# Split-weight rings of four tiles and a second raw ring in the up projections

## The chip, the cores and the metric

The kernel runs on one core of a Trainium2 chip. The metric is the time of one execution on the device in microseconds (us), the median of several runs; smaller is better. The core has a matrix engine (TensorE, PE in the profile), a vector engine (VectorE, DVE), a scalar engine (ScalarE, ACT), GpSimd (POOL, hardly used here) and SyncE (SP), which here issues DMA loads. Each engine works off its own instructions in order; semaphores hold an instruction until what it needs is there.

## The reference

Two layers of a transformer-like trunk on a sequence of 1024 tokens, width 1024, in float32. Layer 0 mixes tokens with a gated short convolution, layer 1 with latent attention; both have the same kind of MLP, and the change lies in its first half:

```python
def squared_relu_mlp(h, w_up, w_down):      # w_up 1024 x 4096, w_down 4096 x 1024
    return jnp.square(jax.nn.relu(h @ w_up)) @ w_down

for l in range(DEPTH):                      # DEPTH = 2
    ...
    h = modulate(rmsnorm(x, norm_g[l, 2]), sh_f, sc_f)
    y = squared_relu_mlp(h, mlp_up_w[l], mlp_down_w[l])
    x = x + g_f[:, None, :] * rmsnorm(y, norm_g[l, 3])
```

## The kernel before

All large products run on TensorE in a reduced float format, and each float32 operand is split in two halves: `hi` is the rounded copy (ScalarE, `split_w`, L176) and `lo` the rest (VectorE, L177). A product takes three matmuls per 128 x 512 tile (`mm`, L173): lo by hi, hi by lo, hi by hi.

The up projection `h @ w_up` is worked off in 16 pairs of 128-column blocks of `w_up`. A pair is a 2 x 2 block product by Winograd's form of Strassen's scheme: seven block products in place of eight. Each block product is four tiles deep, so it is 12 matmuls. In the code the products have numbers. A later pair (`begun is None`) runs first the blocks "11" and "21", then P6, P7, P5, P3 and P4; that makes 84 matmuls. For the pairs 0 to 4 (`AHEAD = 5`), the products "11" and "21" have been done ahead, in `first_pairs`, while the residual of the previous stage was still being finished, and five products, 60 matmuls, are left. Pair 0 is worked off wholly in `first_pairs`, under an order written out by hand (`ORDER`, inside `pinned()`, which fixes the order on all engines but SP); the pairs 1 to 15 run in `all_pairs`.

What a pair needs in tiles:

- Two raw weight tiles a and b (128 x 1024 float32, 4 KB a partition), loaded by `load_pair` through SP. They come from `raw_tile()`, a ring of four that is shared with everything else that is loaded: the residual's tiles in the stage before, the modulation weights `ada_w` (`ada_acc`, L198, run in the background by `run_bg`), the activations of the next stage.
- Split tiles `uphi` and `uplo` from `up_split`, rings of three each in the pool `up`. `pair_sums` makes in this order: two differences and sums on VectorE in the raw tiles (L526, L527), the split t2 of raw tile b, the difference L531, the split s2 (its own pair of half-size tiles, one buffer), the difference L534, and the split t3 of raw tile a. A later pair makes one more split, of the unmodified a. P6 uses s2, P5 and P4 use t2, P7 and P3 use t3. A raw tile is free when its last split has been made, a split tile when its last product has run.
- PSUM banks: `x_` collects P6, P5 and P3 in this order, `v` P7 and P4. Between two of these, what is in `x_` must be taken out (`take`): on VectorE in L580 for the pairs 1 to 4, on ScalarE in L578 for the later ones. P3 and P4 of a pair are kept back in the list `end` and run within the next pair (`second`, `fourth`); a later pair runs them after its products "11" and "21", whereas the pairs 2 to 4 run them after their own P6.

Outside of `pinned()` blocks a planner of the framework puts the instructions of each engine in order before the program runs: by the order of the program, and by when it reckons that operands, tiles and buffers will be ready. A ring's size therefore decides both how long an instruction waits on the chip and where the planner puts it. The results of a pair are squared and combined (`store`, `sums`, L1189 to L1207) and stored to the DRAM tiles `ha` or `hd` for the down projection.

The pool `up` is opened in `down_phase` (used with `pairs=True` in front of both up projections, and with `pairs=False` in front of the attention, where `up` carries the weights of the query and key projections) and released at the end of `mlp_up`; the down projection (`down_pairs`) then lays its weight tiles over that place.

Of the kernel before, what the change touches and what calls it, by code (L numbers as in the profile page):

```python
# [8 lines left out]
F32 = mybir.dt.float32  # L9
F32R = mybir.dt.float32r  # L10
# [7 lines left out]
P = 128  # L18
D = 1024
S = 1024  # L20
KD = D // P
# [14 lines left out]
AHEAD = 5  # L36
# [25 lines left out]
def trunk_kernel(ctx: ExitStack, tc: tile.TileContext, x, c, ada_w, ada_b, norm_g, conv_in_w, conv_w,  # L62
# [5 lines left out]
    def nm(s):  # L68
        uid[0] += 1
        return f"{s}_{uid[0]}"  # L70
# [32 lines left out]
    def raw_tile():  # L103
        return rawp.tile([P, D], F32, tag="raw", name=nm("raw"), bufs=4)
# [4 lines left out]
    def row_tile():  # L109
        return yp.tile([P, D], F32, tag="y", name=nm("y"), bufs=NT)  # L110
# [15 lines left out]
    def ld(out_, in_):  # L126
        nc.sync.dma_start(out_, in_)
# [47 lines left out]
    def split_w(hi, lo, src):  # L175
        nc.scalar.activation(hi, src, AF.Copy)  # L176
        nc.vector.tensor_tensor(lo, src, hi.bitcast(F32), op=ALU.subtract)  # L177
# [328 lines left out]
        return up_split(up, r3, kk)  # L506

    def up_split(up, r3, kk=KD):
        hi = up.tile([P, KD, P], F32R, tag="uphi", name=nm("uphi"), bufs=3)
        lo = up.tile([P, KD, P], F32R, tag="uplo", name=nm("uplo"), bufs=3)  # L510
        split_w(hi[:, :kk, :], lo[:, :kk, :], r3[:, :kk, :])
        return hi, lo


    def load_pair(w, i):
        raws = []
        for f in (2 * i, 2 * i + 1):
            raw = raw_tile().rearrange("p (k m) -> p k m", k=KD)
            ld(raw, w[:, f * P:(f + 1) * P].rearrange("(k p) m -> p k m", p=P))
            raws.append(raw)  # L520
        return raws
# [22 lines left out]
    def halves(t):  # L544
        return t[:, :HALF], t[:, HALF:]
# [97 lines left out]
    def first_pairs(seam, acts, up, wmat, ws, ops):  # L643

        acts = {**acts, **seam.acts(PLAIN)}
        tiles, ca, wl, rest, out_, seen = {}, {}, {}, {}, {}, {}

        def late(i):
            wl[i] = ad.tile([P, D], F32, tag="acc", name=nm("w"), bufs=1).rearrange("p (k m) -> p k m", k=KD)
            ld(wl[i], wmat[:, 2 * i * P:(2 * i + 1) * P].rearrange("(k p) m -> p k m", p=P))  # L650

        def narrow():
            if not tiles:
                banks(True)
                tiles.update({i: bank_ps() if i > 1 else mm_ps() for i in range(AHEAD)})

        def first(i):
            narrow()
            prod(tiles[i], (ws[i], 0, "11"), ops)

        def first_out(i):
            ca[i] = row_tile()
            nc.scalar.activation(ca[i][:, HALF:], tiles[i], AF.Copy)

        def second(i):
            prod(tiles[i], (ws[i], 4, "21"), ops, False)

        def second_out(i):
            nc.scalar.activation(ca[i][:, :HALF], tiles[i], AF.Relu)

        def high(r3, part_=None):
            hi, lo = part_ or (up.tile([P, KD, P], F32R, tag="uphi", name=nm("uphi"), bufs=3),
                               up.tile([P, KD, P], F32R, tag="uplo", name=nm("uplo"), bufs=3))
            nc.scalar.activation(hi, r3, AF.Copy)
            return hi, lo

        def low(w, r3):
            nc.vector.tensor_tensor(w[1], r3, w[0].bitcast(F32), op=ALU.subtract)

        def split_late(i):  # L680
            low(ws[i], wl[i])
            if i + 1 < AHEAD:
                late(i + 1)

        for i in range(AHEAD):
            acts[f"fi{i}"] = lambda i=i: first(i)
            acts[f"ev1_{i}"] = lambda i=i: first_out(i)
            acts[f"se{i}"] = lambda i=i: second(i)
            acts[f"ev2_{i}"] = lambda i=i: second_out(i)
            acts[f"spa{i}"] = lambda i=i: ws.append(high(wl[i]))  # L690
            acts[f"spd{i}"] = lambda i=i: split_late(i)
        late(3)
        a, b = load_pair(wmat, 0)
        a11, a12, a21, a22 = a[:, 0:4, :], a[:, 4:8, :], b[:, 0:4, :], b[:, 4:8, :]
        sums = {}

        def diff(dst, x_, y_, op=ALU.subtract):
            nc.vector.tensor_tensor(dst, x_, y_, op=op)

        def begin():  # L700
            diff(a11, a11, a21)
            diff(a21, a21, a22, ALU.add)

        def s2():
            sums["s2"] = high(a21, tuple(up.tile([P, 4, P], F32R, tag="s2" + "hl"[i], name=nm("s2"), bufs=1) for i in range(2)))

        acts["S1"] = begin
        acts["t2a"] = lambda: sums.update(t2=high(b))
        acts["t2d"] = lambda: low(sums["t2"], b)
        acts["S2"] = lambda: diff(a21, a22, a11)  # L710
        acts["s2a"] = s2
        acts["S3"] = lambda: diff(a12, a12, a21)
        acts["s2d"] = lambda: low(sums["s2"], a21)
        acts["t3a"] = lambda: sums.update(t3=high(a))
        acts["t3d"] = lambda: low(sums["t3"], a)

        def piece(j, kk):
            w, k0, name = {5: ("t2", 0, "t1"), 4: ("t2", 4, "t4"), 6: ("s2", 0, "t2"), 7: ("t3", 0, "t3"), 3: ("t3", 4, "22")}[j]
            if j not in out_:
                out_[j] = mm_ps() if j in (5, 6) else bank_ps()  # L720
            seen[j] = seen.get(j, 0) + 1
            w = sums[w]
            mm(out_[j], (w[0][:, k0 + kk, :], w[1][:, k0 + kk, :]), ops[name][kk], seen[j] == 1, seen[j] == 4)

        for j in (3, 4, 5, 6, 7):
            for kk in range(4):
                acts[f"p{j}_{kk}"] = lambda j=j, kk=kk: piece(j, kk)

        with pinned():
            for name in ORDER:  # L730
                acts[name]()
            p1, cb = ca[0][:, HALF:], row_tile()
            c21, c22 = halves(cb)
            nc.vector.tensor_tensor(c21, p1, out_[6], op=ALU.add)
            nc.vector.tensor_tensor(c22, c21, out_[5], op=ALU.add)
            nc.vector.tensor_tensor(c21, c21, out_[4], op=ALU.add)
            nc.vector.tensor_tensor(p1, c22, out_[3], op=ALU.add)
            nc.vector.tensor_tensor(c22, c22, out_[7], op=ALU.add)
            nc.vector.tensor_tensor(c21, c21, out_[7], op=ALU.add)
        return [ca[i] for i in range(AHEAD)], cb  # L740
# [415 lines left out]
    def down_phase(slots, sizes, wd, src_fn, g, xsrc, xdst, next_w, key, ys=None, pairs=True):  # L1156

        begun = ys is not None
        ys = ys or [row_tile() for _ in range(NT)]
        up = pool("up", "right")  # L1160
        ws = []
        seam = Seam(nx, ys, vtile[g], xsrc, xdst)
        if pairs:
            names = ("11", "21", "22", "t1", "t2", "t3")
            hs = {n: as_quarter(slots[i]) for n, i in zip(names, (2, 3, 0, 1, 4, 5))}
            hs["t4"] = {}
            acts, steps0 = quarter_steps(ys, key, hs), None
            wcols = [next_w[:, 2 * i * P:(2 * i + 1) * P] for i in range(3)]
        else:
            hs = [as_h(slots, H0), as_h(slots, H1)]  # L1170
            steps0, steps1 = h_steps(tp, ys, 0, key, hs[0]), h_steps(tp, ys, 1, key, hs[1])
            wcols = [next_w[:, i * P:(i + 1) * P] for i in range(3)]
        down(slots, sizes, wd, src_fn, ys, seam, steps0, 0, lambda: ws.extend(up_weights(up, [w]) for w in wcols), begun)
        if pairs:
            return up, ws, hs, first_pairs(seam, acts, up, next_w, ws, hs), ys
        return up, ws, hs, first_block(seam, steps0, steps1, ws, hs[0]), ys

    def mlp_up(l, up, ops, firsts, per_pair_bg):

        ca, cb = firsts  # L1180
# [34 lines left out]
        def between(i):  # L1215
            flush()
            if i >= AHEAD:
                run_bg(per_pair_bg)

        store(0, ca[0], cb)  # L1220
        end = all_pairs(up, ops, [(lambda i=i: load_pair(mlp_up_w[l], i), ca[i] if i < AHEAD else None, quarter,
                                   lambda a, b, i=i: store(i, a, b), lambda i=i: between(i)) for i in range(1, n)])
        second, fourth = end.pop(), end.pop()
        second()
# [6 lines left out]
    def cols_of(w, n):  # L1231
# [5 lines left out]
    up, ws, hs, firsts, _ = down_phase(slots, (2, 2, 4), conv_out_w[0], from_dram(hd), "g0m", x0, xs[0],  # L1237
                                      mlp_up_w[0], "0f")
# [9 lines left out]
    up, ws, hs, firsts, ys = down_phase(slots, (ROWS,), mlp_down_w[0], from_dram(hd), "g0f", xs[0], xs[1], q_a_w[0], "1m", ys=ys,  # L1248
                                       pairs=False)
# [253 lines left out]
    for h in range(H):  # L1503
# [58 lines left out]
        if more:  # L1562
            keys(K2, kw, h + 1, 0)
            queries(Q2, qw_, 0)
            if h % 2:
                rotary(R2, qw_, 0)
                V2 = {}
                for b in range(4):
# [17 lines left out]
    up, ws, hs, firsts, _ = down_phase(slots, (2, 2, 4), attn_o_w[0], from_dram(hd), "g1m", xs[1], xs[2],  # L1586
                                      mlp_up_w[1], "1f")
# [52 lines left out]
```

## Time and profile before

| | us |
|---|---|
| median of 3 runs | 2179.61 (2178.7 to 2180.36) |
| the profiled execution | 2180.9 |
| its span, first to last instruction | 2179.1 |
| TensorE busy | 2098.4 (96%) |
| VectorE busy | 1512.0 (69%) |
| ScalarE busy | 1062.7 (49%) |

The mean granted clock of TensorE is 0.993 of full speed. The DMA queue of loads moved 248.57 MB. In the rows of the profile a name like `uplo<-raw,uphi` gives what an instruction writes and reads, by the names of the program's tiles; x121 is a count; "idle before" is the time in which the engine stood still just before such instructions, and what ended it. `raw` is a raw weight tile, `uphi` and `uplo` the split tiles, `s` the split s2, `y` a row tile with results, `one`, `mm` and `tp` PSUM banks, `slot` and `q` the split activations.

### The profile page before, as it was taken

The numbers are of one execution on the slowest core, as the hardware profiler recorded it, in microseconds if no ns is written. First come the engines' busy times: TensorE is split into PE (matmuls) and PEld (weight loads), VectorE is DVE, ScalarE is ACT, GpSimd is POOL, SyncE is SP. The second block draws the span as 40 slices with busy tenths as digits, with TensorE's granted clock in tenths as the row PEclk, the third lists the DMA queues.
The fourth block names the chain that finished last, engine by engine and source line by source line (L and its number), as shares of the span: only waits on it lengthen the run. The fifth ranks groups of instructions, "written<-read, shape, count | busy, mean of one in ns | idle before, by whom it ended". The sixth has DMA issues, their size and how long they took to land.

```text
span 2179.1 us, 25354 instructions
## 1 busy us (share of the span) xinstructions
PE 2098.4 (96%) x9702; PEld 1726.9 (79%) x9702; DVE 1512.0 (69%) x2001; ACT 1062.7 (49%) x1512; POOL 4.0 (0%) x8
## 2 busy tenths in 40 slices
PE   6999999989999999999899999999989999999998
PEld 5888878768888778888777888877768887788887
DVE  5877776967665578956788776665966665458556
ACT  4533354735454434344665555564735444444342
POOL 0000000000000000000000000000000000000000
PEclk9999999999999999999999999999999999999999
DMA  8344463346543977444224131053345553853243
GB/s 243 101 147 134 145 212 127 101 146 203 184 160 120 330 262 254 167 147 170 78 69 122 66 113 44 25 164 122 98 149 174 183 188 119 312 196 126 97 145 135
DMA packets 242335, 330.95 MB, mean 152 GB/s; under 512 B 18629, under 2 KB 143906, under 8 KB 242214
## 3 DMA queue, kind: packets, MB, share of 16 engines
q1 hardware_dynamic: 204328, 248.57, 35.8%
q10 hardware_dynamic: 37886, 80.77, 9.8%
q8 instruction: 76, 1.25, 0.2%
q14 instruction: 45, 0.37, 0.1%
HBM read 248.55 MB, written 80.74 MB: 151 GB/s over the span
## 4 chain that ended last, share of the span: by engine, by line
PE 69%; DVE 14%; ACT 8%; DMA 6%; issue 2%; SPq 0%; ACTq 0%; DVEq 0%
PE one L173 34%; PE mm L173 18%; PE tp L173 7%; PE big L173 4%; DMA raw<-in_ada_w_dram 3%; ACT junk L258 2%; PE big L1433 2%; DVE y L318 1%; DVE raw L319 1%; DVE acc L198 1%; PE tp L1459 1%; DVE uplo L177 1%; DMA raw<-ha 1%; DVE y L312 1%; ACT small L260 1%
## 5 line engine op out<-in xcount | busy, mean ns | idle before, releaser
L173 PE MATMUL one<-slot,uphi 128*128 128x512 f32 x1240 | 383.9, 391 | 0.0
L173 PEld LDWEIGHTS one<-slot,uphi 128*128 128x128 f32 x1240 | 233.8, 189 | 48.6 <-issue 0.5
L173 PE MATMUL big<-slot 128*128 128x512 f32 x1152 | 266.5, 391 | 1.0 <-ACT y L884 0.6
L173 PE MATMUL one<-slot,uplo 128*128 128x512 f32 x620 | 244.1, 394 | 14.6 <-DVE y L580 12.6
L173 PEld LDWEIGHTS big<-slot 128*128 128x128 f32 x1152 | 215.9, 188 | 46.7 <-ACT y L884 1.4
L173 PE MATMUL one<-ring,ring 128*128 128x512 f32 x1008 | 232.3, 391 | 6.5 <-DVE ring L177 6.5
L177 DVE TENSOR_TENSOR uplo<-raw,uphi 128x1024 fp32r<-128x1024 f32 x121 | 145.8, 1221 | 130.5 <-ACT uphi L176 130.5
L176 ACT ACTIVATE ring<-w 128x1024 fp32r<-128x1024 f32 x98 | 103.7, 1058 | 261.7 <-PE tp L173 132.1
L173 PEld LDWEIGHTS one<-ring,ring 128*128 128x128 f32 x1008 | 188.2, 188 | 49.5 <-ACT ring L176 5.8
L176 ACT ACTIVATE uphi<-raw 128x1024 fp32r<-128x1024 f32 x121 | 128.2, 1060 | 143.8 <-PE one L173 91.6
L177 DVE TENSOR_TENSOR ring<-w,ring 128x1024 fp32r<-128x1024 f32 x98 | 119.8, 1222 | 109.7 <-ACT ring L176 109.6
L173 PE MATMUL mm<-ring,ring 128*128 128x512 f32 x672 | 162.4, 390 | 0.0
L173 PE MATMUL tp<-ring,ring 128*128 128x512 f32 x672 | 161.7, 389 | 0.0
L173 PE MATMUL mm<-slot,uphi 128*128 128x512 f32 x504 | 158.5, 395 | 0.0
L173 PEld LDWEIGHTS one<-slot,uplo 128*128 128x128 f32 x620 | 116.8, 188 | 43.6 <-DVE y L580 15.1
L173 PEld LDWEIGHTS mm<-ring,ring 128*128 128x128 f32 x672 | 125.7, 188 | 27.1 <-DVE ring L177 0.6
L173 PEld LDWEIGHTS tp<-ring,ring 128*128 128x128 f32 x672 | 126.2, 188 | 26.2
L198 DVE SCALAR_TENSOR_TENSOR acc<-raw,csil,acc 128x1024 f32<-128x1024 f32 x88 | 112.8, 1282 | 45.7 <-DMA raw<-in_ada_w_dram 42.2
L177 DVE TENSOR_TENSOR ring<-raw,ring 128x1024 fp32r<-128x1024 f32 x98 | 119.4, 1219 | 18.3 <-ACT ring L176 18.3
L173 PE MATMUL one<-slot,s 128*128 128x512 f32 x468 | 115.1, 395 | 3.7 <-DVE s L177 3.7
L578 ACT ACTIVATE y<-one 128x512 f32<-128x512 f32 x62 | 36.7, 592 | 159.3 <-PE one L173 104.7
L173 PEld LDWEIGHTS mm<-slot,uphi 128*128 128x128 f32 x504 | 95.3, 190 | 20.3 <-issue 1.4
(278 smaller groups left out, 3498.4 us busy)
## 6 DMA issues: line engine op xcount, KB each, us to landing
ha<-y ACTq DMA_DIRECT2D x196, 256.0 KB, 3.6
raw<-ha SPq DMA_DIRECT2D x98, 512.0 KB, 4.2
raw<-in_ada_w_dram SPq DMA_DIRECT2D x80, 512.0 KB, 4.5
raw<-in_mlp_up_w_dram SPq DMA_DIRECT2D x70, 512.0 KB, 4.2
w<-in_mlp_down_w_dram SPq DMA_DIRECT2D x56, 512.0 KB, 4.9
raw<-hd SPq DMA_DIRECT2D x24, 512.0 KB, 5.3
xs<-raw ACTq DMA_DIRECT2D x24, 512.0 KB, 2.9
raw<-xs SPq DMA_DIRECT2D x24, 512.0 KB, 3.2
```

The source lines that it names most:

```text
L173: nc.tensor.matmul(out_, lhs[a], rhs[b], start=first and i == 0, stop=last and i == 2, skip_group_check=more)
L176: nc.scalar.activation(hi, src, AF.Copy)
L177: nc.vector.tensor_tensor(lo, src, hi.bitcast(F32), op=ALU.subtract)
L198: nc.vector.scalar_tensor_tensor(acc, raw, s, acc, op0=ALU.mult, op1=ALU.add)
L258: nc.scalar.activation(junk, src, AF.Square, accum_out=ss)
L260: nc.scalar.activation(rt, ss, AF.Sqrt, bias=eps_d)
L312: nc.vector.tensor_tensor(y, y, p_, op=ALU.add)
L318: nc.vector.scalar_tensor_tensor(y, y, rroot(ss), self.gmb, op0=ALU.mult, op1=ALU.mult)
L319: nc.vector.tensor_tensor(xr, xr, y, op=ALU.add)
L578: nc.scalar.activation(dst, x_, AF.Copy)
L1433: nc.tensor.matmul(o_, a, m_, start=j == 0, stop=j == 4 and b * HALF + w < n)
L1459: nc.tensor.transpose(p_[:, c:c + P], pts[4 * hf + i][:, j * P:(j + 1) * P], ident)
```

## The change

In `down_phase` the size of the two split rings is set by a variable: four tiles each (`uphi`, `uplo`) where an up projection follows (`pairs`), three as before in the stage before the attention. The up-like products of the convolution, which run before `down_phase` is first called, keep three. `load_pair` gets the pool `up` from the two up projections; for every pair whose number can be divided by 3 (0, 3, 6, 9, 12, 15) the two raw tiles are taken from a ring of two in `up` and not from the common ring of four. The convolution's pairs don't pass the pool and keep the common ring. The pool grows by 16 KB a partition: two more split tiles and two raw tiles of 4 KB each. No instruction is added or taken away.

```diff
--- before.py
+++ after.py
@@ -506,16 +506,19 @@
         return up_split(up, r3, kk)
 
     def up_split(up, r3, kk=KD):
-        hi = up.tile([P, KD, P], F32R, tag="uphi", name=nm("uphi"), bufs=3)
-        lo = up.tile([P, KD, P], F32R, tag="uplo", name=nm("uplo"), bufs=3)
+        hi = up.tile([P, KD, P], F32R, tag="uphi", name=nm("uphi"), bufs=depth[0])
+        lo = up.tile([P, KD, P], F32R, tag="uplo", name=nm("uplo"), bufs=depth[0])
         split_w(hi[:, :kk, :], lo[:, :kk, :], r3[:, :kk, :])
         return hi, lo
 
 
-    def load_pair(w, i):
+    depth = [3]
+
+    def load_pair(w, i, up=None):
         raws = []
         for f in (2 * i, 2 * i + 1):
-            raw = raw_tile().rearrange("p (k m) -> p k m", k=KD)
+            raw = up.tile([P, D], F32, tag="raw", name=nm("raw"), bufs=2) if up and i % 3 == 0 else raw_tile()
+            raw = raw.rearrange("p (k m) -> p k m", k=KD)
             ld(raw, w[:, f * P:(f + 1) * P].rearrange("(k p) m -> p k m", p=P))
             raws.append(raw)
         return raws
@@ -669,8 +672,8 @@
             nc.scalar.activation(ca[i][:, :HALF], tiles[i], AF.Relu)
 
         def high(r3, part_=None):
-            hi, lo = part_ or (up.tile([P, KD, P], F32R, tag="uphi", name=nm("uphi"), bufs=3),
-                               up.tile([P, KD, P], F32R, tag="uplo", name=nm("uplo"), bufs=3))
+            hi, lo = part_ or (up.tile([P, KD, P], F32R, tag="uphi", name=nm("uphi"), bufs=depth[0]),
+                               up.tile([P, KD, P], F32R, tag="uplo", name=nm("uplo"), bufs=depth[0]))
             nc.scalar.activation(hi, r3, AF.Copy)
             return hi, lo
 
@@ -690,7 +693,7 @@
             acts[f"spa{i}"] = lambda i=i: ws.append(high(wl[i]))
             acts[f"spd{i}"] = lambda i=i: split_late(i)
         late(3)
-        a, b = load_pair(wmat, 0)
+        a, b = load_pair(wmat, 0, up)
         a11, a12, a21, a22 = a[:, 0:4, :], a[:, 4:8, :], b[:, 0:4, :], b[:, 4:8, :]
         sums = {}
 
@@ -1156,6 +1159,7 @@
     def down_phase(slots, sizes, wd, src_fn, g, xsrc, xdst, next_w, key, ys=None, pairs=True):
 
         begun = ys is not None
+        depth[0] = 4 if pairs else 3
         ys = ys or [row_tile() for _ in range(NT)]
         up = pool("up", "right")
         ws = []
@@ -1218,7 +1222,7 @@
                 run_bg(per_pair_bg)
 
         store(0, ca[0], cb)
-        end = all_pairs(up, ops, [(lambda i=i: load_pair(mlp_up_w[l], i), ca[i] if i < AHEAD else None, quarter,
+        end = all_pairs(up, ops, [(lambda i=i: load_pair(mlp_up_w[l], i, up), ca[i] if i < AHEAD else None, quarter,
                                    lambda a, b, i=i: store(i, a, b), lambda i=i: between(i)) for i in range(1, n)])
         second, fourth = end.pop(), end.pop()
         second()
```

## The prediction, made before the changed kernel ran

> **What bounds the kernel now.** I read the page first, then the table by stages, then who waits for whom on TensorE, then the chain of waits through the place that the table points to.
>
> ```profile
> span 2179.1 us, 25354 instructions
> PE 2098.4 (96%) x9702; PEld 1726.9 (79%) x9702; DVE 1512.0 (69%) x2001; ACT 1062.7 (49%) x1512; POOL 4.0 (0%) x8
> ```
>
> The first line is the span, the second the engines' busy time. TensorE is busy 96% of the span, so a change that leaves the matmuls alone can win only where TensorE waits or runs slowly. The change touches the two up projections. The table by stages, with the beginning and the long part of the first one, then of the second, then two closer looks at the first:
>
> ```profile
> core 0: us, PE busy (x) PEld busy (x) DVE busy (x) ACT busy (x) POOL busy (x), PEclk, DMA share, GB/s
> 446.00:500.00 54.00, 47.62 (x200) 38.45 (x201) 31.18 (x43) 18.78 (x21) 0.00 (x0) 0.97 0.49 161
> 500.00:700.00 200.00, 200.00 (x881) 164.92 (x880) 125.54 (x167) 100.89 (x125) 0.00 (x0) 1.00 0.48 159
> 1590.35:1644.35 54.00, 47.86 (x201) 38.66 (x202) 29.84 (x42) 18.66 (x21) 0.00 (x0) 0.97 0.46 153
> 437.00:446.00 9.00, 8.49 (x36) 6.68 (x36) 8.75 (x14) 5.26 (x6) 0.00 (x0) 1.00 0.66 201
> 464.60:470.50 5.90, 5.83 (x18) 4.64 (x19) 1.82 (x4) 0.08 (x1) 0.00 (x0) 0.71 0.33 90
> ```
>
> In the long part of the stage (200 us) TensorE never stops: 881 matmuls in 200.00 us is 0.227 us each. There is nothing to gain there. Just before it, in 54 us, 200 matmuls are done, which at that pace need 45.4 us: 8.6 us are lost. In the second stage 201 matmuls need 45.7 of 54 us: 8.3 us are lost. Together 16.9 us, and that is the ceiling of what these places can give. The last row shows a part of the loss that is no waiting: behind the longest wait 18 matmuls, worth 4.1 us, take 5.9 us at a granted clock of 0.71, so 1.8 us go to the clock. Who ends the waits, in the first stage (two rows) and in the second:
>
> ```profile
> PE one L173 <- DVE y L580: 6.4, 3, 4.0
> PE one L173 <- DVE s L177: 1.6, 1, 1.6
> ```
>
> ```profile
> PE one L173 <- DVE y L580: 6.2, 3, 3.8
> ```
>
> Three waits per stage for L580, a VectorE addition that takes a sum out of PSUM so that TensorE may go on adding into that bank. This form of the step exists only for the pairs 1 to 4 (those begun early); later pairs use ScalarE for it and have another product in between. Why L580 comes late stands in the chain of waits, in order of time (start, us, what):
>
> ```profile
> 446.00 0.70 DVE y L580
> ...
> 452.48 0.02 issue
> 452.50 1.07 ACT uphi L176
> ...
> 453.60 1.24 DVE uplo L177
> ...
> 454.86 6.05 DMA raw<-in_mlp_up_w_dram
> ...
> 460.98 0.69 DVE raw L526
> 461.68 1.14 DVE uplo L177
> 462.81 0.60 DVE raw L527
> 463.41 0.60 DVE raw L531
> 464.02 0.61 DVE y L580
> ...
> 464.67 7.38 PE one L173 x24
> ...
> 481.17 0.61 DVE y L580
> ```
>
> This is the whole case in one column. At 452.48 TensorE finishes the last use of a split tile (P3 of pair 1). Only then can ScalarE write the next split into it (the wait for a split tile, 3 of them 15.0 us below), VectorE finishes the split at 454.84, which frees a raw tile, only then is the raw weight of pair 4 loaded (6.05 us), and VectorE stands at L526 of pair 4 with the L580 of pair 2 queued four instructions behind it. So both rings are in the chain that ended last: three split tiles and four raw tiles.
>
> ```profile
> ACT uphi L176 <- PE one L173: 15.0, 3, 7.4
> ```
>
> **The change part by part.** Nothing is added to or taken from the work: the same splits, the same 70 raw loads, the same matmuls. Only where tiles lie and when they come free is different.
>
> *Raw tiles of its own for pairs 0, 3, 6, ...* Pair 0 leaves the ring of four and pair 3 follows it in its own two tiles. Pair 4 then takes the ring tiles of pair 1, not of pair 2. In the trace the tiles of pair 1 are those that come free for these two loads:
>
> ```profile
> 436.24 1.57 SPq L127 DMA_DIRECT2D raw<-in_mlp_up_w_dram x2
> ```
>
> So pair 4's loads can be issued by 437.8 in place of 454.86, and with even the 6.05 us of the chain they land by 443.9, 17 us ahead of L526 at 460.98. The DMA term leaves the chain. Loads that are issued earlier queue on SP ahead of others; SP has nothing else that TensorE waits for until the weights of the next stage.
>
> *Fourth split tile.* Pairs 1 to 4 need two splits each, t2 (from raw tile b) and t3 (from a). With three tiles the t2 of pair i+1 waits for the end of P4 of pair i-1; with four it takes the tile that P3 leaves, 12 matmuls (2.7 us) before. From there the split of s2, which P6 of pair i+1 needs, is five steps away: 1.07 + 1.24 + 0.60 (L531) and two half-size splits. Half-size I take from the rows below as half of 1060 and 1221 ns, 1.1 us together (an estimate). That makes 4.0 us, and between that release and the end of P5 of pair i lie P4, P7 and P5, 36 matmuls or 8.2 us. So at the second and third boundary P6 of the next pair is ready when TensorE comes to it, its 12 matmuls cover L580, and no wait is left: neither the 4.0 nor the third one (before 481.17 and behind it, the rest of the 6.4, about 1.6 us). If that cover fails, a wait of about 0.75 us is left, the bare time of L580 (0.70 at 446.00, and the semaphore).
>
> ```profile
> L177 DVE TENSOR_TENSOR uplo<-raw,uphi 128x1024 fp32r<-128x1024 f32 x121 | 145.8, 1221 | 130.5 <-ACT uphi L176 130.5
> L176 ACT ACTIVATE uphi<-raw 128x1024 fp32r<-128x1024 f32 x121 | 128.2, 1060 | 143.8 <-PE one L173 91.6
> ```
>
> [...]
>
> *What stays or comes back.* The first boundary (446) follows nine microseconds in which VectorE is busy 8.75 of 9.00; more tiles don't make VectorE faster, so I keep its 0.75 us and a restart, 0.95 us per stage, 1.9 in all. The 1.6 us wait for s is set by s2, which has one buffer before and after; it lies ahead of 446 and stays. With tiles free earlier the planner may move work of pairs 1 to 3 (L526, L527, a split's low half) into this full stretch of VectorE, ahead of results that TensorE waits for. Bounds: 0, where nothing moves in front, and one low half with L526 and L527, 1.22 + 2 x 0.6 = 2.4 us per stage. I take 1.0 per stage, 2.0 in all, nearer to the lower end since most of that work stands before 446 already. A gain below nothing is possible too, in the joins of the earlier stages where the raw ring is shared with the residual's tiles; the trace shows no wait of TensorE that a raw tile ends there, so 0 to 1 us.
>
> *Entry of the next stage.* The pool of split tiles grows by 16 KB a partition, so the tiles that the down projection lays over it change. By the order in which that stage makes its tiles, those that lie there are the blocks 22 and 21 of the down weights, loaded after its first product, so I cost it at nothing. Were the first weights laid over the last split tile, one load (4.9 us) would stand open per stage.
>
> ```profile
> w<-in_mlp_down_w_dram SPq DMA_DIRECT2D x56, 512.0 KB, 4.9
> ```
>
> *Sum.* 16.9 - 1.9 - 2.0 = 13.0 us less. The profiled execution took 2180.9 us (its span of 2179.1 and 1.8 around it), so 2167.9 for it; it lies 1.3 us above the median of the runs, 2179.6, so 2166.6 for the median. With the bounds, 16.9 + 1 down to 16.9 - 1.9 - 4.8 = 10.2, the forecast's own range is 2161.7 to 2169.4.
>
> **The rivals.** *Half of it.* The DMA goes but the planner keeps its order, and L580 stays bare at all three boundaries: 0.95 us x 3 x 2 = 5.7 us are kept, with each of the six L580 one more VectorE instruction late (0.6 x 6 = 3.6), and with the 2.0 the gain is 16.9 - 5.7 - 2.0 - 3.6 = 5.6 us, 2174.0. For it: L580 at 481.17 was late with no DMA in its chain. Against: the 8.2 us against 4.0.
>
> *No change.* The stretch before 446 is VectorE's, not the tiles'. If about 8 us per stage of splits and sums move in front of it, TensorE waits there instead of at 464: 2179.6. For it: 8.75 of 9.00. Against: between 446 and 500 VectorE is busy 31 of 54 us and has room where the work stands now. [...]
>
> *Slower.* In the long part ScalarE has a margin that can be used up. These are its rows in one pair, and the matmul that follows:
>
> ```profile
> 505.56 2.17 ACT L176 ACTIVATE uphi<-raw 128x1024 fp32r<-128x1024 f32 x2
> ...
> 515.10 0.60 ACT L578 ACTIVATE y<-one 128x512 f32<-128x512 f32 x1 [4.85 <-PE one L173]
> ```
>
> ```profile
> 517.34 0.39 PE L173 MATMUL one<-slot,uplo 128*128 128x512 f32 x1
> ```
>
> L578 frees the bank that P3 adds into, and ends at 515.70, 1.64 us before the group of 517.34. With a free split tile the planner can put two whole splits (2.17 us) ahead of L578. Up to 1.64 us of such delay costs nothing; beyond it, it counts in 11 pairs of both stages, 22 times. It eats the gain of 13.0 from 0.6 us per pair on, 2.2 us of ScalarE work in front. With another full activation of 1.06 us behind the two splits it is 3.2 - 1.64 = 1.6 us; I take 1.0, which gives 22.0 - 13.0 = 9 us more, 2188.6. Against it: ScalarE idles 4.85 us before L578, so the splits must start very late to be in the way.
>
> **How the numbers follow.** About 0.2%, 4.4 us, is what a measurement of this kernel can tell from no change. Forecast 0.62, half of it 0.13, no change 0.12, slower 0.13. Half of it straddles the bound by little, so faster is 0.74 (nearly all of the first two), same 0.13, slower 0.13. The likeliest is 2166.6. The range takes in the forecast's bounds and reaches over half of it to just past no change: 2161.5 to 2181.0; the slower case and the tail of the third are left out.
>
> **What would show it.** In the profile after, the table by stages should have the 54 us windows (moved with the stage) shortened to about 47 us of work for 200 matmuls, at a granted clock of 1.00; the waits of TensorE for L580 at one per stage, under 1 us; no DMA of the raw weights in the chain there; the 200 us window still full. A row of TensorE waiting on ScalarE's L578 in the long part, or on VectorE before 446, would make the forecast wrong, as would a wait at the entry of the down stage longer than now.

## The result and the profile after

| | before | changed |
|---|---|---|
| median, us | 2179.21 (2175.83 to 2181.37, 8 runs) | 2171.85 (2170.21 to 2174.38, 8 runs) |
| the profiled execution | 2180.9 | 2171.63 |

The ratio is 0.9969, interval 0.9959 to 0.9979: faster by 7.4 us, where 13.0 were forecast. In the changed kernel line numbers from the ring sizes on are three higher (L580 is L583, L526 is L529). The page counts 46 instructions fewer, but none of them is work of an engine: the counts of matmuls and of VectorE's and ScalarE's instructions are the same.

The first lines of the page, then the table by stages: the 54 us from P6 of pair 1 on in both stages, the long part, and a closer look at the 6 us behind that P6.

```profile
span 2169.8 us, 25308 instructions
PE 2098.7 (97%) x9702; PEld 1729.0 (80%) x9702; DVE 1524.6 (70%) x2001; ACT 1061.4 (49%) x1512; POOL 4.0 (0%) x8
```

```profile
440.70:494.70 54.00, 53.93 (x232) 44.59 (x233) 40.29 (x56) 25.11 (x28) 0.00 (x0) 0.97 0.63 207
500.00:700.00 200.00, 200.00 (x881) 164.91 (x880) 127.81 (x163) 98.46 (x123) 0.00 (x0) 1.00 0.45 150
1579.80:1633.80 54.00, 53.92 (x231) 44.46 (x232) 39.64 (x56) 24.74 (x28) 0.00 (x0) 0.97 0.60 195
440.70:446.70 6.00, 5.93 (x20) 4.85 (x21) 4.51 (x8) 4.62 (x5) 0.00 (x0) 0.74 0.87 260
```

These windows begin with P6 of pair 1; those shown of the kernel before began three products later. From P6 of pair 1 on (437.40 and 1581.80), the kernel before had 198 and 199 matmuls in 54 us; the changed one has 232 and 231, and TensorE has next to no idle time. What is missing to a full pace (54 us are 238 matmuls at 0.227 us) is the clock: 0.74 in the first six microseconds. The long part is as before, 881 matmuls in 200 us. The waits of TensorE, first stage (two rows), then the second:

```profile
PE one L173 <- DVE s L177: 4.1, 1, 4.1
PE big L173 <- ACT y L887: 1.9, 1, 1.9
```

```profile
PE one L173 <- DVE s L177: 4.2, 1, 4.2
```

The waits for L580 (6.4 and 6.2 us) are gone from both lists. In their place the wait for the split s of pair 1, which was 1.6, is 4.1 and 4.2, and a wait in the convolution's out projection for a copy on ScalarE, at 308.74, is 1.9. In the kernel before it was 0.4:

```profile
PE big L173 <- ACT y L884: 0.4, 1, 0.4
```

The chain of waits shows what stands in front of the first:

```profile
432.59 4.41 DMA raw<-in_mlp_up_w_dram
...
437.09 0.69 DVE raw L529
437.79 0.59 DVE y L737
438.38 1.14 DVE uplo L177
439.52 0.60 DVE y L738
440.12 0.61 DVE s L177
...
440.77 29.33 PE one L173 x122
```

A raw load is again in the chain, though not the one of before: it is pair 2's, and VectorE stands at the first difference of pair 2 with the split s of pair 1, which TensorE wants, queued behind it. VectorE's timeline in the changed kernel, and the same piece of work in the kernel before:

```profile
426.41 0.69 DVE L529 TENSOR_TENSOR raw<-raw,raw 128x512 f32<-128x512 f32 x1 [0.55 <-DMA raw<-in_mlp_up_w_dram]
...
428.83 0.69 DVE L529 TENSOR_TENSOR raw<-raw,raw 128x512 f32<-128x512 f32 x1
...
434.18 0.69 DVE L530 TENSOR_TENSOR raw<-raw 128x512 f32<-128x512 f32 x1
...
437.09 0.69 DVE L529 TENSOR_TENSOR raw<-raw,raw 128x512 f32<-128x512 f32 x1 [0.90 <-DMA raw<-in_mlp_up_w_dram]
...
440.03 0.68 DVE L177 TENSOR_TENSOR s<-raw,s 128x512 fp32r<-128x512 f32 x1
```

```profile
425.01 0.68 DVE L526 TENSOR_TENSOR raw<-raw,raw 128x512 f32<-128x512 f32 x1
...
434.99 1.23 DVE L177 TENSOR_TENSOR uplo<-raw,uphi 128x1024 fp32r<-128x1024 f32 x1 [1.28 <-ACT uphi L176]
...
436.73 0.69 DVE L177 TENSOR_TENSOR s<-raw,s 128x512 fp32r<-128x512 f32 x1
```

The rows at 426.41 and 425.01 are the first difference of pair 1. In the changed kernel three differences of other pairs have moved in front of s: two of pair 3 (428.83 and 434.18), whose weights are there because they have tiles of their own, and one of pair 2 (437.09). Three differences are 1.8 us, one addition more (L738, an addition of pair 0's results) 0.6, the wait for pair 2's load 0.90, and the 1.28 us that VectorE stood idle before are used up: 2.0 more. By the rows, the way from the first difference to s is 13.62 us in place of 11.72, so 1.9 more. With the 0.55 for pair 1's load that is 2.5, which is the growth of TensorE's wait, from 1.57 to 4.12. In the second stage the same work has moved; there it is 0.69 for pair 1's load and 2.0 more behind it.

Where the time went along the program, by the start of the same matmul in each trace (the last columns belong to the first experiment below):

| matmul | before | changed | difference | four split tiles only | difference |
|---|---|---|---|---|---|
| first of the convolution's out projection | 296.49 | 295.76 | -0.73 | 296.01 | -0.48 |
| first of up stage 0 | 389.55 | 390.34 | +0.79 | 389.06 | -0.49 |
| P6 of pair 1 | 437.47 | 440.77 | +3.30 | 436.80 | -0.67 |
| P6 of pair 6 | 525.50 | 521.16 | -4.34 | 516.92 | -8.58 |
| second stage, first | 1533.81 | 1529.15 | -4.66 | 1523.22 | -10.59 |
| second stage, P6 of pair 1 | 1581.86 | 1579.88 | -1.98 | 1570.99 | -10.87 |
| second stage, P6 of pair 6 | 1669.64 | 1660.52 | -9.12 | 1651.12 | -18.52 |
| end of the span | 2179.1 | 2169.8 | -9.3 | 2160.4 | -18.7 |

From P6 of pair 1 to P6 of pair 6 the changed kernel gains 7.64 and 7.14 us. Ahead of it, from the first matmul of each up stage on, it loses 2.51 and 2.68, and 1.52 more between 296 and 389. Between the two stages, where nothing is changed, it gains 0.3, and the kernel of the first experiment gains 2.0: so much can differ between single executions elsewhere.

### The profile page after: what moved, and what is told of

The parts are those of the page before. It is cut to its first block, busy times and chain, and to the rows that moved or that the text cites. A ratio compares the mean times of both kernels' runs of the same rounds, so it can differ in the third digit from the quotient of the medians.

```text
span 2169.8 us, 25308 instructions
## 1 busy us (share of the span) xinstructions
PE 2098.7 (97%) x9702; PEld 1729.0 (80%) x9702; DVE 1524.6 (70%) x2001; ACT 1061.4 (49%) x1512; POOL 4.0 (0%) x8
## 4 chain that ended last, share of the span: by engine, by line
PE 72%; DVE 13%; ACT 7%; DMA 6%; issue 2%; ACTq 0%; SPq 0%; DVEq 0%
PE one L173 36%; PE mm L173 18%; PE tp L173 7%; PE big L173 5%; DMA raw<-in_ada_w_dram 3%; PE big L1437 2%; ACT junk L258 2%; DVE y L318 1%; DVE raw L319 1%; DVE acc L198 1%; PE tp L1463 1%; DMA raw<-in_mlp_up_w_dram 1%; DVE y L312 1%; DMA raw<-ha 1%; DVE small L1440 1%
## 5 line engine op out<-in xcount | busy, mean ns | idle before, releaser
L198 DVE SCALAR_TENSOR_TENSOR acc<-raw,csil,acc 128x1024 f32<-128x1024 f32 x88 | 112.8, 1282 | 46.6 <-DMA raw<-in_ada_w_dram 43.7
L173 PEld LDWEIGHTS one<-slot,s 128*128 128x128 f32 x468 | 91.0, 195 | 29.4 <-DVE s L177 10.1
```

Of the source, the lines that this page charges most:

```text
L173: nc.tensor.matmul(out_, lhs[a], rhs[b], start=first and i == 0, stop=last and i == 2, skip_group_check=more)
L198: nc.vector.scalar_tensor_tensor(acc, raw, s, acc, op0=ALU.mult, op1=ALU.add)
```

## The experiments

All medians stand beside runs of the kernel before on the same chip, 2178.66 in the first group, 2179.06 in the second, 2179.28 in the third.

**One half each.** First four split tiles, with every raw tile from the common ring; then the own raw tiles, with three split tiles.

```diff
-            raw = up.tile([P, D], F32, tag="raw", name=nm("raw"), bufs=2) if up and i % 3 == 0 else raw_tile()
+            raw = up.tile([P, D], F32, tag="raw", name=nm("raw"), bufs=2) if False else raw_tile()
```

> Only the fourth split tile; all raw tiles from the common ring of four as before the change. The question is why TensorE's wait for s of pair 1 grew from 1.6 to 4.1 us per stage. Theory A (order): pair 3's own raw tiles are there early, so the planner puts the differences of pairs 3 and 2 (L529, L530) ahead of the low half of s of pair 1 on VectorE. It expects the wait at 1.6 us here, no wait for the take-out addition (L583, L580 before) of more than 0.8 us, no late start at 308 us, and a time of 2163 to 2166. Theory B (split tiles): the fourth tile lets more splits of pair 1 stand ahead of s; it expects the wait at 4.1 here and a time of 2170 to 2172. Theory C (transfers): the raw weights land late because the pairs' loads crowd; it expects 1.6 here, as A does, since the loads are as before.

```diff
-        depth[0] = 4 if pairs else 3
+        depth[0] = 3
```

> Only the raw tiles of their own for pairs 0, 3, 6, ...; split rings of three. A and C: the wait for s of pair 1 is 4.1 us per stage as after the change, with the clock lowered behind it; the waits for the take-out addition remain at about 0.8 us each, since the split tiles still come late, but the 4.0 us one with its transfer is gone. Loss of 8.2 and 1.5, gain of 16.9 - 5.7 = 11.2: 2176 to 2179. B: wait for s at 1.6 us, time 2167 to 2169.

The first took 2161.96 us (2159.56 to 2163.27, 5 runs), ratio 0.9924 [0.9911, 0.9937]; the second 2177.17 (2173.49 to 2180.16, 11 runs), 0.9994 [0.9985, 1.0002]. The fourth split tile alone gives 16.7 us, a little more than was expected; with the own raw tiles added, it is 7.4. The own raw tiles alone cannot be told from the kernel before. The waits of TensorE in the first stage, of the first kernel and then of the second:

```profile
PE one L173 <- DVE s L177: 1.4, 1, 1.4
...
PE one L173 <- DVE y L583: 0.8, 1, 0.8
```

```profile
PE one L173 <- DVE s L177: 4.3, 1, 4.3
PE big L173 <- ACT y L887: 2.8, 1, 2.8
PE one L173 <- DVE y L583: 2.4, 2, 1.6
```

With four split tiles alone the wait for s is as short as before, and no late start stands at 308; theories A and C both expect that, and B is out. The own raw tiles alone bring both new waits; they do take away the 4.0 us wait for L583, but two of up to 1.6 us stay. So the longer wait for s comes from the raw tiles, not from more split tiles, and the load of pair 4 that stood in the chain of before had no need of tiles of its own: once the splits are done earlier, the common ring is free earlier. With four split tiles alone SP issues it at 448.38, in place of 454.86:

```profile
448.38 0.37 SPq L127 DMA_DIRECT2D raw<-in_mlp_up_w_dram  x1
```

**Is it the order on VectorE?** The changed kernel, with an order alone added: the first two differences of a pair stand behind the low half of the split s of the pair before, whose name `mark` holds. No wait is added. (Here and below only the lines that matter are shown.)

```diff
+        for x_, y_, z_, op in ((a11, a11, a21, ALU.subtract), (a21, a21, a22, ALU.add)):
+            nc.vector.tensor_tensor(x_, y_, z_, op=op)
+            if mark and depth[0] == 4:
+                tc.add_manual_dep(last_dve(), mark[-1], NO_SYNC, reason="behind s2")
```

> The whole change, with an order on VectorE: the first two differences of pair i may stand only behind the split s2 of pair i-1. No wait for data is taken away or added. The loads are those of the changed kernel. A: the wait for s of pair 1 falls back to about 1.6 us in both stages, the waits for the take-out addition stay away, and with the 1.5 us at 308 us still there the time is 2163 to 2166. C: the raw tiles land as late as after the change, so the wait stays above 2.5 us and the time at 2170 to 2172.

And the changed kernel with pair 0's raw weights in the common ring:

```diff
-... if up and i % 3 == 0 else raw_tile()
+... if up and i and i % 3 == 0 else raw_tile()
```

> The whole change, but pair 0 takes its raw tiles from the common ring; pairs 3, 6, ... have tiles of their own. Both rings are larger. The planner's VectorE order ahead of s of pair 1 is then that of the kernel before. A: wait for s 1.6 us, no late start at 308 us (pair 0's weights are not loaded ahead of the convolution's output weights), 2161 to 2165. B: 4.1 us and 2170 to 2172.

They took 2165.75 us (2164.37 to 2168.64, 5 runs), ratio 0.9946 [0.9934, 0.9958], and 2162.87 (2161.09 to 2168.92, 6 runs), 0.9935 [0.9922, 0.9947]. In both the wait for s is 1.4 again; first the ordered kernel (its L895 is the copy of L887), then the other:

```profile
PE big L173 <- ACT y L895: 2.1, 1, 2.1
PE one L173 <- DVE s L177: 1.4, 1, 1.4
...
PE one L173 <- DVE q L458: 1.1, 1, 1.1
```

```profile
PE big L173 <- ACT y L887: 2.9, 1, 2.9
PE one L173 <- DVE s L177: 1.4, 1, 1.4
```

The order of VectorE is shown as the cause of the 4.1 us: same tiles, same loads, another order, and it is gone. So theory C, late transfers, is out too. The second kernel's expectation missed the place at 308, where no late start was expected and one of 2.9 us stands: now it is pair 3's loads that find their tiles free at once and go out between the loads of the out projection:

```profile
292.21 2.83 SPq L127 DMA_DIRECT2D raw<-in_mlp_up_w_dram  x2
```

This run shows one thing more. Pair 3's weights are there even earlier than in the changed kernel, and yet VectorE does none of its differences before s of pair 1: s starts at 438.13, the first difference of another pair at 439.34. So early weights alone do not move the work. Why the planner moves it in the changed kernel and not here is open.

**Is the late start at 308 the early loads?** The changed kernel, with pair 0's loads behind the last load of the out projection on SP:

```diff
+            if up and i == 0 and hmark:
+                tc.add_manual_dep(last_sp(), hmark[-1].name, NO_SYNC, reason="behind hd")
```

> The changed kernel, with pair 0's two raw loads kept on SP behind the last load of the earlier projection's hd (an order only; no wait is added). Everything else, VectorE's order before the first boundary too, is as in the changed kernel. Theory (the early loads at 295.5 push the next conv_out load back, which lands 2.9 us late for ScalarE): the wait of TensorE for the copy of y at 308.74 falls from 1.94 to about 0.4, the 4.1 us waits for s of pair 1 stay, and the median is 1.5 us lower than the changed kernel's 2171.85, about 2170.3. Rival (the wait at 308 comes from where tiles lie or when they come free, not from SP's queue): the wait stays at 1.9 or more and the median at 2171.9.

2170.44 us (2168.88 to 2172.49, 6 runs), ratio 0.9961 [0.9948, 0.9973]. SP's queue and ScalarE in the changed kernel:

```profile
295.50 1.47 SPq L127 DMA_DIRECT2D raw<-in_mlp_up_w_dram  x2
...
301.94 0.33 SPq L127 DMA_DIRECT2D raw<-in_conv_out_w_dram  x1
```

```profile
305.44 1.06 ACT L176 ACTIVATE slot<-raw 128x1024 fp32r<-128x1024 f32 x1 [2.92 <-DMA raw<-in_conv_out_w_dram]
```

and the waits of the experiment:

```profile
PE one L173 <- DVE s L177: 4.1, 1, 4.1
...
PE big L173 <- ACT y L894: 0.2, 1, 0.2
```

The wait at 308 is 0.2 (L894 is the copy of L887 here) and the one for s untouched, as the theory says. The medians of the two kernels, 1.4 us apart, don't tell them apart by themselves (their intervals overlap); the row does.

**Both orders, then a third.** Both orders together:

> Both orders at once: the loads of pair 0 held behind the last hd load, and on VectorE the first two differences of pair i behind the split of the sum of pair i-1. All that the change allots (four split tiles, own raw tiles) stays. Theory (the own raw tiles cost only by those two changes of order): the waits for s are 1.4 us, the one at 308 is 0.4, and the median is that of the version with four split tiles alone, 2162 (2160.5 to 2163.5). Rival (own raw tiles cost in a third way too, by transfers or by places): it stays at 2165 or above, though both waits are gone.

2165.77 us (2162.63 to 2167.73, 6 runs), ratio 0.9939 [0.9924, 0.9953]: not the 2162 of the theory but the 2165 or above of the rival, though both waits were short. By the medians, holding pair 0's loads back gave nothing on top of the order on VectorE (2165.75 and 2165.77, on two chips). What was left stands on VectorE at the first difference of pair 1 (L542 is L529 here):

```profile
425.00 0.69 DVE L542 TENSOR_TENSOR raw<-raw,raw 128x512 f32<-128x512 f32 x1 [0.97 <-DMA raw<-in_mlp_up_w_dram]
```

On SP the first own-tile load of pair 3 was ahead of pair 1's two. The last kernel puts it behind them, and beside it the version with four split tiles alone ran again:

```diff
+            if up and i == 3:
+                tc.add_manual_dep(last_sp(), pmark[1], NO_SYNC, reason="behind pair 1")
```

> As the run with both orders (2165.77), and on SP the own-tile loads of pair 3 stand behind both loads of pair 1 instead of the first of them ahead (an order only). In that run VectorE's first difference of pair 1 waits 0.97 us for its raw load at 425.00, and TensorE then 1.5 us for q at 432.43, where the version with four split tiles alone waits 0 and 0.4. Theory (the rest of the own raw tiles' cost is pair 3's load in front of pair 1's): that wait for the load is under 0.3 us, the one for q about 0.5 in both stages, and the kernel is within 1.5 us of the version with four split tiles alone run beside it. Rival (there is a cost of another kind, or the difference of 3.8 us was spread of the runs with nothing behind it but this 1 us per stage): the waits go as said and it stays 3 us or more above; or the waits don't go.

> The version with four split tiles and all raw weights from the common ring once more, beside the run with three orders, so that the two are compared on one chip: 2160.5 to 2163.5.

2163.34 us (2160.92 to 2165.14, 5 runs), ratio 0.9925 [0.9913, 0.9938], against 2162.25 (2160.64 to 2163.59, 5 runs), 0.9920 [0.9906, 0.9933]. VectorE's row (L546 is L529 here) and TensorE's wait in the kernel with three orders:

```profile
424.36 0.69 DVE L546 TENSOR_TENSOR raw<-raw,raw 128x512 f32<-128x512 f32 x1
```

```profile
PE one L173 <- DVE q L458: 0.4, 1, 0.4
```

With three orders put right, the whole change, tiles and all, is as fast as four split tiles alone, within what these runs can tell. So the own raw tiles cost by order, on VectorE and on SP (twice), and gain nothing that these runs show. The third order is shown by its rows only: the waits went as its theory says, but the interval of this kernel overlaps that of the one with two orders.

**More of the same.** Four split tiles only, with two buffers for s2; and five split tiles.

```diff
-name=nm("s2"), bufs=1)
+name=nm("s2"), bufs=2 if depth[0] == 4 else 1)
```

> Four split tiles and all raw weights from the common ring (2161.96), and the sum's split s2 in two buffers instead of one. What is left in that kernel at the first boundary are waits of 1.4 us for s and 0.8 us for L583 per stage. Theory (they are VectorE's work: it is busy 8.75 of the 9.00 us before): the waits stay within 0.5 us of that and the median at 2161 to 2163. Rival (they are the one buffer of s2, free only when P6 of the pair before has ended): the 1.4 us goes, in both stages, and the median is 2158 to 2159.5.

```diff
-        depth[0] = 4 if pairs else 3
+        depth[0] = 5 if pairs else 3
```

> Five split tiles in place of four, all raw weights from the common ring. Theory (four are enough: no wait for a split tile is left in the chain of the boundaries): within 0.1% of the version with four, 2160 to 2164, the same waits. Rival (as with the own raw tiles, more room lets the planner put splits in front of what TensorE waits for next): the waits for s or for L583 grow by 2 us per stage or more, 2166 or above. Second rival (a fifth tile still takes away a wait): 2159 or below.

2160.28 us (2158.96 to 2160.76, 5 runs), ratio 0.9913 [0.9900, 0.9926], and 2162.96 (2161.59 to 2164.84, 6 runs), 0.9926 [0.9914, 0.9938]. With two buffers the wait for s of pair 1 is gone in both stages, so it was the one buffer and not VectorE, against the theory written down; the wait for L583 stays and a new one of 0.6 and 1.1 us stands ahead of it, for an addition of pair 0's results (L739) on VectorE. The median is 1.7 us lower than with one buffer, less than the 2.5 to 4 of the rival. In the first stage:

```profile
PE one L173 <- DVE y L583: 0.8, 1, 0.8
...
PE one L173 <- DVE y L739: 0.6, 1, 0.6
```

It is the fastest kernel here by its median, but its interval overlaps that of four split tiles alone. A fifth split tile gives nothing: the same waits of 1.4 and 0.8 in both stages.

## Why the prediction was right in its direction and too high in its size

*The ceiling and the kept boundary held, the latter by luck.* 16.9 less 1.9 was to be won from the boundaries. No run shows the restart of 0.20 us that stands in each 0.95 of the 1.9 beside the 0.75; in the kernel before, behind the wait that ends at 446.75, the first three matmuls take 0.80 us from the start of the first to the start of the fourth, in place of 0.68, so 0.12. The change gained 7.64 + 7.14 = 14.8 from P6 of pair 1 on; four split tiles alone 7.91 + 7.65 = 15.6, with one bare L583 of 0.8 us per stage left, as forecast. In the changed kernel it is luck that the sum comes so near to 15.0. The bare L583 is gone there, since TensorE comes later, but behind the longer wait for s the clock is lowered (20 and 19 matmuls in 6 us, at 0.74 and 0.72, in place of 26), which costs about 1.5 us per stage and was not in the sum.

*The two steps were one.* The prediction had the DMA leave the chain by the own raw tiles and the split tile by the fourth buffer. The runs show that the fourth tile does both, so the loads that the own raw tiles made earlier had nothing left to win.

*Moved VectorE work: the term that was mis-sized.* 1.0 per stage was taken, 2.0 in all, from bounds of 0 to 2.4 per stage. Measured: 2.51 and 2.68 ahead of P6 of pair 1, both above the upper bound. Of these 1.9 and 2.0 are VectorE's; 0.55 and 0.69 are the wait for pair 1's load, which is SP's. The mechanism was named down to its instructions (differences moved in front of what TensorE waits for); but I chose from the lower end because most such work stood ahead of 446 anyway, which says nothing about pair 3's, and I left out the wait for a load with which a moved instruction can stand in the queue (0.90 and 1.02). The "no change" rival's mechanism was at work for a part, 3.9 of its 16 us.

*SP: the claim that was wrong.* "SP has nothing else that TensorE waits for" was looked at from 436 on. Pair 0's own tiles are free from the moment the pool opens, and its loads went out at 295.50, among the loads of the stage before: 1.52 us. And pair 3's first load into an own tile went out ahead of pair 1's: the 0.55 and 0.69 above. The same view of SP, taken at the pool's opening, would have shown the out projection's loads there.

*The sum.* 14.8 - 5.2 - 1.5 = 8.1; with the 0.7 by which the changed execution was ahead at 296, the 0.3 between the stages and 0.2 at the end it is the 9.3 between the two profiled executions. The one of before lay 1.7 above the median of all its runs and the one after 0.2 below its own, so 7.4 between the medians.

*The signs.* The waits for L580, forecast at one per stage, were none. The long part stayed full, no wait for ScalarE's L578 arose (the slower rival), the down stage's entry cost nothing (its first matmuls are as far ahead as the last of the stage). A raw load was in the chain after all, ahead of the first boundary, and the clock there is 0.74, not 1.00; the windows themselves came out as said (232 matmuls in 54 us are 200 in 46.6). Above all, TensorE waits longer on VectorE ahead of 446 (the 4.1 and 4.2 us for s), a row that the prediction's own list names as making the forecast wrong. The list named the right place: about a third of what the boundaries gave was lost again there.

## What to carry to other kernels

Under a planner that orders by when operands are there, a deeper buffer is not free even where memory is: it can move work, loads and instructions both, ahead of what the critical engine waits for. Give one more buffer at a time, take the one whose release stands in the chain, and look at the chain again before giving the next; where an early load has to be kept, fix its place in each queue that it passes. For the forecast: look at each queue from the moment that a new tile is free, not from where the old wait stood.

## What the runs showed of the hardware

The longest waits of TensorE in the up stages cost more than their length. After each of the four waits of 3.8 to 4.2 us in the kernels before and after (up to 464.67 and 1608.83, and up to 440.77 and 1579.88), 5 to 7 matmuls came 427 ns apart instead of 227, and in the 6 us from the end of the wait 19 or 20 matmuls ran in place of 26, which is 1.4 to 1.6 us more. With shorter waits the length did not decide. The waits of 1.4 to 1.6 us for s at P6 of pair 1 were followed by a clock of 1.00, with 26 matmuls in 6 us, in both stages of the kernel before and in the first with four split tiles alone. At about 280 us, in the convolution, TensorE waits for another s: 0.57 us in the kernel before, 0.87 in the changed one, 0.18 with four split tiles alone and 1.74 with five. In all four traces the granted clock (the third number from the end of a window's row) is at 0.50 by 1.6 us after the end of the wait; in the kernel before it is 0.50 from 281.60 to 284.60, in the changed one from 280.00 to 283.30. The shortest of these waits and its window, with four split tiles alone, then the longest, with five:

```profile
279.68 1.66 PE L173 MATMUL one<-slot,s 128*128 128x512 f32 x6 [0.18 <-DVE s L177]
```

```profile
281.20:284.60 3.40, 3.40 (x10) 2.62 (x9) 3.40 (x5) 1.73 (x3) 0.00 (x0) 0.50 0.97 383
```

```profile
280.53 2.93 PE L173 MATMUL one<-slot,s 128*128 128x512 f32 x6 [1.74 <-DVE s L177]
```

```profile
280.50:286.50 6.00, 5.97 (x14) 4.71 (x15) 5.28 (x6) 1.75 (x3) 0.00 (x0) 0.50 0.87 301
```

And a wait of 2.0 us in the attention stage, which no change here touches, is followed by a lower clock in the kernel before (2.03 us; 16 matmuls in the 4 us from 1082.10 on, at 0.69) and in the changed one, but not with four split tiles alone. The changed kernel, then the other:

```profile
1078.48 0.66 PE L173 MATMUL mm<-slot,uplo 128*128 128x512 f32 x1 [2.02 <-ACT lat L1277]
```

```profile
1078.40:1082.40 4.00, 3.92 (x15) 3.13 (x15) 2.24 (x4) 2.33 (x5) 0.00 (x0) 0.57 0.72 224
```

```profile
1073.29 0.50 PE L173 MATMUL mm<-slot,uplo 128*128 128x512 f32 x1 [2.02 <-ACT lat L1277]
```

```profile
1073.20:1077.20 4.00, 3.91 (x23) 3.34 (x24) 3.17 (x6) 3.24 (x7) 0.00 (x0) 1.00 0.69 212
```

These are 15 matmuls in 4 us against 23, at 0.57 and 1.00. The length of the wait does not order these cases: the clock fell behind a wait of 0.18 us at one place and did not behind 1.4 to 1.6 us at another, and behind the same wait of 2.02 us it fell in one execution and not in the other. What decides is not shown. For the comparison of two kernels: from the end of that wait to the next matmul with `uplo` it is 2.02 us in the changed kernel (1078.48 to 1080.50) and 1.15 with four split tiles alone (1073.29 to 1074.44), so 0.87 us between two single executions came with the lower clock in a stage that neither change touches.
